# The prologue of a two-block network on one core, put into a fixed order: norm row spread by a product, first weight chunk ahead of token tile 1, decay logarithms after the prologue

## The chip, the core and the metric
The kernel runs on one core of a Trainium2 chip. Its five engines each work through a queue of their own in order: TensorE (PE, matrix products, with PEld for the loads of its stationary operand), VectorE (DVE), ScalarE (ACT), GpSimd (POOL) and SyncE (SP), which here does nothing but issue DMA transfers. The metric is the device time of one execution in microseconds (us); lower is better.

## The reference
256 tokens of width 1024 go through two different transformer blocks. All is float32. Only the first stage of the first block matters here: an RMS norm, a projection of the normed tokens with `w_in` (1024 x 3072), dilated window attention on one half of its columns, and retention on the other half.

```
def rms_norm(x, w, eps=NORM_EPS):
    xf = x.astype(jnp.float32)
    y = xf * lax.rsqrt(jnp.mean(xf * xf, axis=-1, keepdims=True) + eps)
    return (y * w.astype(jnp.float32)).astype(x.dtype)
...
def parallel_mixer(h, w_in, q_norm_w, k_norm_w, decay_f, decay_b, gn_w, w_out):
    proj = h @ w_in
...
    lg_f = jax.nn.log_sigmoid(decay_f.astype(f32))
    lg_b = jax.nn.log_sigmoid(decay_b.astype(f32))
    y_f = retention_chunkwise(qr, kr, vr, lg_f, inclusive=True)
...
x = x + parallel_mixer(rms_norm(x, norm_mix_w[l]), w_in[l], ...)
x = x + memory_cross_attention(...)
x = x + hierarchical_moe(...)
```

After it come a cross attention on a memory, a mixture of 32 experts (its weights are some 200 MB), and the second block: feed-forward, four-way mixer, feed-forward, twice.

## The kernel before, in words
The tokens are two tiles of 128 (`x[0]`, `x[1]`; tile 0 is called t0 here, tile 1 t1). A float32 product is made of three fast products: each operand is split into a high part and the remainder (`xh`, `xl` for the tokens, `wh`, `wl` for the weights), and `mm3` multiplies high by high, and each remainder by the other's high part (L310, L311, L312).

Weights come in chunks of 128 x 2048 elements (1 MB) through a ring of four buffers `raw`, in the order in which they are used. Each chunk has two halves of 1024 columns. For a half, ACT copies the high part (`wh`, L279) and DVE or POOL subtracts it (`wl`, L283). A counter `nw` in `weight` says who subtracts: POOL for each fourth half, DVE otherwise; the list `on_pool` overrules it (before, it sends both halves of the first chunk to POOL). The pools of `wh` and `wl` hold three halves each, so the high part of a half waits until TensorE has done with the half three before it.

`dense_nat` is one projection of both token tiles by 512 columns: two chunks, 2 tiles x 8 k-steps x 3 products = 48 matmuls of 128x128 by 512 columns. The first three are the keys, queries and values of the attention (chunks 0 and 1, 2 and 3, 4 and 5). When a key or query tile is done, `kdone` or `qdone` norms it by head (ACT square, DVE sum, POOL power -0.5 `rq`, DVE multiply) and TensorE transposes it (L401).

The prologue is `mixer1`: 18 products of zeros (`WARM`) keep TensorE busy while the loads run; SP issues x of t0 in two halves, the identity, x of t1, the norm row `norm_mix_w` copied from memory to all 128 partitions (0.5 MB into the core), and chunk 0 in two halves (512 KB each). Each tile is scaled by its 1/rms and the norm row (L530), transposed in two groups of four (L401) and split (L391, L392). `retention_start` then loads a row and the eight decays, and `log_decay` turns the decays into logarithms by a chain of some twenty small DVE operations, each waiting for the one before.

The framework's scheduler sets the order on each engine, except where `manual_schedule` takes the order of the code, and where `issue_after` ties one instruction behind another. Two groups of small constants are loaded meanwhile: for the router (`wr`, `tri`; POOL multiplies `wr`, DVE casts `tri`), and for a mixer of the second block (`bc_diff_lambda_2`, in `lambdas`: POOL product `lm`, DVE sum `ls`, ACT exponential). SP has eight completion semaphores (`DMAHW0` to `DMAHW7`) which it takes in turn, so an issue waits until the transfer eight before it has landed.

## Time and profile before

| | |
|---|---|
| median of 3 runs | 1740.98 us (1739.96 to 1743.69) |
| profiled execution, its own time | 1743.4 us |
| its span in the trace | 1741.7 us |
| TensorE busy | 1576.9 us (91%) |
| VectorE, ScalarE, GpSimd busy | 840.0, 656.5, 286.5 us |
| DMA moved | 419.07 MB |

The profile is of one execution; its own time is 1.7 us more than its span, and 2.4 us more than the median of the runs. A busy TensorE is not TensorE at its peak. Idle time of an engine costs only where another waits for it.

### The profile page before, as it was taken

The page shows a single profiled execution, that of the slowest core. Times are in us where ns is not written, and L with a number is a line of the kernel's source. Part 1 is how long each engine was busy: PE and PEld are TensorE (multiplying, and loading weights), DVE is VectorE, ACT ScalarE, POOL GpSimd, SP SyncE. Part 2 cuts the span into 40 slices and gives each one's busy share as a digit, 9 for nine tenths or more (in the row PEclk, how much of TensorE's full clock was granted, in tenths as well). Part 3 has the DMA queues.
Part 4 walks back from the last instruction along what each step waited for, and adds up shares of the span by engine and source line. Part 5 has one row for each costly group of instructions (what it writes and reads, how often), then busy time and mean ns, then how long its engine had stood idle before and what let it go on. Part 6 is the DMA issues. An engine that isn't in the chain of part 4 may idle for free.

```text
span 1741.7 us, 24950 instructions
## 1 busy us (share of the span) xinstructions
PE 1576.9 (91%) x10070; PEld 1215.4 (70%) x10070; DVE 840.0 (48%) x1468; ACT 656.5 (38%) x1125; POOL 286.5 (16%) x253
## 2 busy tenths in 40 slices
PE   8998998777776776999999989999999999989998
PEld 6777774322211221799988769999999988779997
DVE  5658653000000000554577775557654677765555
ACT  4655441000000000444545645444444536734442
POOL 4224312100000000312233250000100041330000
PEclk9999998987878886999999989999999999989999
DMA  7454959999999999855543235556455634145551
GB/s 278 149 185 142 359 192 422 417 421 421 420 421 421 421 420 421 318 194 192 195 171 135 79 145 194 184 180 241 148 191 193 243 105 147 50 179 190 179 190 72
DMA packets 66187, 419.07 MB, mean 241 GB/s; under 512 B 10641, under 2 KB 12177, under 8 KB 18705
## 3 DMA queue, kind: packets, MB, share of 16 engines
q1 hardware_dynamic: 66064, 417.39, 63.2%
q8 instruction: 82, 1.34, 0.3%
q14 instruction: 41, 0.33, 0.1%
HBM read 416.32 MB, written 1.05 MB: 240 GB/s over the span
## 4 chain that ended last, share of the span: by engine, by line
PE 63%; DMA 25%; DVE 4%; issue 4%; POOL 3%; ACT 1%; SPq 0%; DVEq 0%; POOLq 0%; ACTq 0%
DMA mraw<-in_wm 23%; PE ps L310 20%; PE ps L312 19%; PE ps L311 19%; PE ps L401 2%; PE ps L480 1%; POOL wl L283 1%; DMA raw<-in_wd 1%; DVE wl L283 1%; POOL rq L418 1%; DVE xa L1234 1%; ACT wh L279 0%; DMA bc_ln_g<-in_ln_g 0%; DVE xl L392 0%; PE ps L991 0%
## 5 line engine op out<-in xcount | busy, mean ns | idle before, releaser
L283 DVE TENSOR_TENSOR wl<-raw,wh 128x1024 fp32r<-128x1024 f32 (+2 forms) x314 | 388.9, 1249 | 292.3 <-ACT wh L279 289.4
L279 ACT ACTIVATE wh<-raw 128x1024 fp32r<-128x1024 f32 (+2 forms) x356 | 370.9, 1052 | 347.3 <-PE ps L311 177.5
L310 PE MATMUL ps<-xh,wh 128*128 128x256 f32 x1424 | 402.1, 282 | 3.4 <-ACT cv L1534 3.4
L312 PE MATMUL ps<-xh,wl 128*128 128x256 f32 x1424 | 401.3, 282 | 0.0
L311 PE MATMUL ps<-xl,wh 128*128 128x256 f32 x1424 | 401.1, 282 | 0.0
L310 PEld LDWEIGHTS ps<-xh,wh 128*128 128x128 f32 x1424 | 268.3, 188 | 7.0 <-ACT cv L1534 3.8
L311 PEld LDWEIGHTS ps<-xl,wh 128*128 128x128 f32 x1424 | 268.4, 188 | 1.8 <-issue 0.4
L312 PEld LDWEIGHTS ps<-xh,wl 128*128 128x128 f32 x1424 | 268.4, 188 | 0.8
L991 PE MATMUL ps<-mraw,xg 128*32 128x512 f32 x1024 | 168.2, 763 | 70.8 <-DMA mraw<-in_wm 70.6
L312 PE MATMUL ps<-wh,xl 128*128 128x512 f32 (+3 forms) x520 | 190.2, 370 | 6.5 <-DVE xl L392 6.3
L310 PE MATMUL ps<-wh,xh 128*128 128x512 f32 (+3 forms) x520 | 190.7, 376 | 4.7 <-ACT xh L391 3.8
L311 PE MATMUL ps<-wl,xh 128*128 128x512 f32 (+3 forms) x520 | 191.9, 370 | 2.2 <-POOL wl L283 1.1
L991 PEld LDWEIGHTS ps<-mraw,xg 128*32 128x32 f32 x1024 | 26.5, 119 | 200.4 <-DMA mraw<-in_wm 164.4
L418 POOL TENSOR_TENSOR rq<-rv,mhalf 128x1 f32<-128x1 f32 (+4 forms) x46 | 46.8, 1017 | 724.6 <-DVE rv L416 721.8
L283 POOL TENSOR_TENSOR wl<-raw,wh 128x1024 fp32r<-128x1024 f32 x42 | 103.2, 2463 | 279.5 <-ACT wh L279 180.4
L997 DVE TENSOR_TENSOR mf<-ps,mf 128x512 f32<-128x512 f32 x8 | 5.5, 692 | 238.7 <-PE ps L991 234.7
L312 PEld LDWEIGHTS ps<-wh,xl 128*128 128x128 f32 x520 | 100.8, 194 | 23.3 <-DVE xl L392 10.4
L310 PEld LDWEIGHTS ps<-wh,xh 128*128 128x128 f32 x520 | 101.0, 195 | 22.1 <-ACT xh L391 7.5
L311 PEld LDWEIGHTS ps<-wl,xh 128*128 128x128 f32 x520 | 101.4, 195 | 17.9 <-POOL wl L283 3.2
L312 PE MATMUL ps<-wh,hf 128*128 128x512 f32 x256 | 100.1, 391 | 0.0
L311 PE MATMUL ps<-wl,hf 128*128 128x512 f32 x256 | 100.1, 391 | 0.0
L310 PE MATMUL ps<-wh,hf 128*128 128x512 f32 x256 | 98.2, 390 | 0.0
(351 smaller groups left out, 1965.2 us busy)
## 6 DMA issues: line engine op xcount, KB each, us to landing
mraw<-in_wm SPq DMA_DIRECT2D x191, 1024.0 KB, 19.8
raw<-in_wd SPq DMA_DIRECT2D x179, 1024.0 KB, 4.9
raw<-in_wd SPq DMA_DIRECT2D x8, 512.0 KB, 11.0
raw<-in_wd SPq DMA_DIRECT2D x4, 832.0 KB, 4.4
bc_ln_g<-in_ln_g SPq DMA_DIRECT2D x6, 512.0 KB, 5.9
bc_ln_b<-in_ln_b SPq DMA_DIRECT2D x6, 512.0 KB, 6.6
raw<-in_wd SPq DMA_DIRECT2D x4, 768.0 KB, 4.4
bias<-in_bias SPq DMA_DIRECT2D x4, 512.0 KB, 6.5
```

Of the source, the lines that this page charges most:

```text
L279: s.nc.scalar.activation(h[:, :n], rc, AF.Copy)
L283: i = eng.tensor_tensor(l[:, :n], rc, h[:, :n].bitcast(F32), op=OP.subtract)
L310: mm(out, lhsT=lh, rhs=rh, start=start, stop=False)
L311: mm(out, lhsT=lh, rhs=rl, start=False, stop=False)
L312: mm(out, lhsT=ll, rhs=rh, start=False, stop=stop)
L401: s.nc.tensor.transpose(ps[:, b * 128:b * 128 + 128], src[:, b * 128:b * 128 + 128], s.ident)
L418: s.last_pow = s.nc.gpsimd.tensor_tensor(q, r, s.mhalf[:, :n], op=OP.pow)
L480: s.nc.tensor.matmul(out, lhsT=v(j), rhs=pt[:, 2 * i + j], start=first and j == 0, stop=last and j == 1)
L991: nc.tensor.matmul(ps[32 * e:32 * e + 32], lhsT=xg[:, k, 32 * e:32 * e + 32], rhs=w[:, e * FF:e * FF + FF], start=k == 0, stop=k == NK - 1 ...
L997: nc.vector.tensor_tensor(f, gu[1], f, op=OP.mult)
L1234: nc.vector.scalar_tensor_tensor(z[:, cs], z[:, cs], mv[:, 0:1], g[:, cs], op0=OP.subtract, op1=OP.mult)
```

## The change
1. The norm row is loaded as one row of 4 KB to one partition, and two products with a row of ones (K = 1, float32) put it on all partitions, in two PSUM banks `wn`. DVE reads it from there. The zeros' products are 14, the two products stand ahead of the last.
2. SP's order is new: x of t0, the row, the identity, the two loads of decays, chunk 0, then x of t1. The row `ret_gn_w` is loaded after the attention's code.
3. `norm1` writes the order of PE, ACT and DVE out by hand: t0's norm, transposes, chunk 0's splits (both `wl` halves now on DVE), 12 products of t0 with chunk 0, then tile 1's norm. The key projection goes on with chunk 1's first half for t0, and then t1.
4. `log_decay` is tied behind the last subtraction of the prologue (`norm1_end`), the product `qk` behind a power.
5. `nw` starts at -4 and the first chunk is not counted, so POOL gets the halves that are second to those it had: another half of each two chunks, up to the first feed-forward.

The core of the diff:

```
-        s.on_pool = [None, None]
+        s.on_pool = []
-        s.nw, s.pool_mod = 0, 4
+        s.nw, s.pool_mod = -4, 4
...
     def dense_nat(..., first=None):
+        if first:
+            w[0] = first(ps[0])
         if stagger:
             for t in range(NT):
-                for c in range(2):
+                for c in range(1 if first and not t else 0, 2):
                     part(t, c)
...
     def mixer1(s):
+                first, r = s.norm1(s.pool(c1, "rms1", side="right"), x, hs, lambda: s.retention_start(ctx))
+                o = s.xsplit()
+                with ExitStack() as c2:
+                    s.dilated(c2, hs, o, first)
+            r["lg"] = s.log_decay(r["p"], r["decay"])
+            r["gnw"] = s.bcast(r["p"], "ret_gn_w", 512)
...
+    def norm1(s, p, x, hs, small):
...
+        for cs in halves:
+            nc.sync.dma_start(x[0][:, cs], s.a["x"][:128, cs])
+        nc.sync.dma_start(row, s.a["norm_mix_w"])
+        nc.sync.dma_start(s.ident, s.a["ident"])
+        r = small()
+        raw = s.raw(cuts=2)
+        nc.sync.dma_start(x[1], s.a["x"][128:])
...
+        def tile(t, between):
+            q = s.rms_scale(z[t], x[t])
+            for c, cs in enumerate(halves):
+                nc.vector.scalar_tensor_tensor(z[t][:, cs], x[t][:, cs], q, wn[c], op0=OP.mult, op1=OP.mult)
+            tp = [s.transpose4(z[t][:, cs]).rearrange("p (b c) -> p b c", b=4) for cs in halves]
+            tk = slice(t * 128, t * 128 + 128)
+            between()
+            for c in range(2):
+                nc.scalar.activation(hs[0][:, 4 * c:4 * c + 4, tk], tp[c], AF.Copy)
+            for c in range(2):
+                h = hs[0][:, 4 * c:4 * c + 4, tk]
+                s.norm1_end = nc.vector.tensor_tensor(hs[1][:, 4 * c:4 * c + 4, tk], tp[c], h.bitcast(F32),
+                                                      op=OP.subtract)
+        def first(out):
+            with order:
+                for i in range(WARM):
+                    if i == WARM - 1:
+                        for c, cs in enumerate(halves):
+                            nc.tensor.matmul(wn[c], lhsT=one, rhs=row[:, cs], start=True, stop=True)
+                    nc.tensor.matmul(ps, lhsT=warm[:, :128], rhs=warm, start=True, stop=True)
+                tile(0, lambda: hi(0))
+                hi(1)
+                lo(0)
+                lo(1)
+                for a, b in ((0, 0), (1, 0), (0, 1)):
+                    for k in range(4):
+                        cs = slice(k % 2 * 512, k % 2 * 512 + 512)
+                        nc.tensor.matmul(out, lhsT=hs[a][:, k, :128], rhs=w[k // 2][b][:, cs], start=a + b + k == 0,
+                                         stop=False)
+                tile(1, lambda: None)
+            return w
...
+        s.issue_after(nc.gpsimd.tensor_tensor(qk, qw, kw, op=OP.mult), s.last_pow)
...
-        nc.vector.scalar_tensor_tensor(na, d, -1.0, d, op0=OP.mult, op1=OP.min)
+        s.issue_after(nc.vector.scalar_tensor_tensor(na, d, -1.0, d, op0=OP.mult, op1=OP.min), s.norm1_end)
```

First place: the head of SP's queue, from the program's start. Before (`raw_125` is chunk 0, `raw_264` chunk 1):

```order
L556 DMA x_91<-in_x 128x512 x2
L557 DMA ident_70<-in_ident 128x128
L558 DMA x_92<-in_x 128x1024
L238 DMA bc_norm_mix_w_123<-in_norm_mix_w 128x1024
L260 DMA raw_125<-in_wd 128x1024 x2
L260 DMA raw_264<-in_wd 128x2048
```

and of the change (`row_102` is the norm row, `raw_236` chunk 1):

```order
L580 DMA x_91<-in_x 128x512 x2
L581 DMA row_102<-in_norm_mix_w 1x1024
L582 DMA ident_70<-in_ident 128x128
L690 DMA decay_118<-in_ret_decay_f 128x4
L690 DMA decay_118<-in_ret_decay_b 128x4
L260 DMA raw_125<-in_wd 128x1024 x2
L585 DMA x_92<-in_x 128x1024 [waits DMAHW0_49]
L260 DMA raw_236<-in_wd 128x2048 [waits DMAHW1_49]
```

The norm row shrinks from 128 rows to one, the decays come ahead of chunk 0, and t1's tokens (`x_92`) behind it.

Second place: SP some transfers later, and DVE at the end of the prologue, where chunk 1's second half is subtracted. SP of the change, from chunk 3 (`raw_358`) on:

```order
L260 DMA raw_358<-in_wd 128x2048 [waits DMAHW7_49]
L666 DMA bias_496<-in_bias1 128x1024 [waits DMAHW0_49]
L666 DMA bias_497<-in_bias1 128x1024 [waits DMAHW1_49]
L238 DMA bc_ret_gn_w_772<-in_ret_gn_w 128x512 [waits DMAHW2_49]
L238 DMA bc_diff_lambda_2_774<-in_diff_lambda_2 128x128 [waits DMAHW3_49]
L867 DMA wr_1861<-in_w_route 128x8x37 [waits DMAHW4_49]
L871 DMA tri_1864<-in_tri 128x128 [waits DMAHW5_49]
```

DVE before, from the subtraction for chunk 1's first half (`wl_267`; its second half stands on POOL) to the first normed key tile (`qn_286`):

```order
L283 TENSOR_TENSOR wl_267<-raw_264,wh_266 128x1024 [waits DMAHW7_49,Activation_49]
L392 TENSOR_TENSOR xl_94<-ps_173,xh_93 128x4x128 [waits Activation_49]
L283 TENSOR_TENSOR wl_355<-raw_352,wh_354 128x1024 [waits DMAHW4_49,Activation_49]
L283 TENSOR_TENSOR wl_359<-raw_352,wh_358 128x1024 [waits Activation_49]
L426 TENSOR_REDUCE hss_288<-qn_286 128x8 [waits Activation_49]
L828 CAST trir_1863<-tri_1859 128x128 [waits DMAHW1_49]
L416 TENSOR_SCALAR rv_290<-hss_288 128x8 [waits DVE_49]
L283 TENSOR_TENSOR wl_389<-raw_386,wh_388 128x1024 [waits DMAHW5_49,Activation_49]
L586 TENSOR_TENSOR qn_286<-ps_242,rq_292 128x512 [waits Pool_49]
```

and of the change, from the prologue's last subtractions to the second half of chunk 1 (`wl_243`):

```order
L604 TENSOR_TENSOR xl_94<-ps_221,xh_93 128x4x128 [waits Activation_49]
L604 TENSOR_TENSOR xl_94<-ps_226,xh_93 128x4x128 [waits Activation_49]
L717 SCALAR_TENSOR_TENSOR lsna_742<-decay_118 128x8
L721 TENSOR_SCALAR lsw_746<-lsz_744 128x8 [waits Activation_49]
L722 RECIPROCAL lsw_746<-lsw_746 128x8 [waits DVE_49]
L723 TENSOR_TENSOR lsw_746<-lsw_746,lsz_744 128x8 [waits DVE_49]
L1259 TENSOR_REDUCE ls_778<-lm_776 128x2 [waits Pool_49]
L725 TENSOR_TENSOR lsw2_750<-lsw_746 128x8 [waits DVE_49]
L727 TENSOR_SCALAR lsacc_752<-lsw2_750 128x8 [waits DVE_49]
L875 CAST trir_1868<-tri_1864 128x128 [waits DMAHW5_49]
L729 TENSOR_TENSOR lsacc_752<-lsacc_752,lsw2_750 128x8 [waits DVE_49]
L283 TENSOR_TENSOR wl_243<-raw_236,wh_242 128x1024 [waits Activation_49]
```

The sum `ls` (behind POOL's `lm`, which waits for `bc_diff_lambda_2`) and the cast of `tri` now stand ahead of `wl_243`; before, the cast stood behind the subtractions for chunks 1 and 2, and the sum behind chunk 4's first half.

Third place: POOL in the retention, around the power `rq` of its first group norm. Before:

```order
L283 TENSOR_TENSOR wl_1658<-raw_1655,wh_1657 128x1024 [waits DMAHW4_49,Activation_49,Pool_49]
L283 TENSOR_TENSOR wl_1692<-raw_1689,wh_1691 128x1024 [waits DMAHW5_49,PE_49,Activation_49]
L283 TENSOR_TENSOR xw_1650<-raw_1733,xw_1650 128x1024 [waits DMAHW0_49,Activation_49]
L418 TENSOR_TENSOR rq_1553<-rv_1551,mhalf_71 128x4 [waits DVE_49]
L283 TENSOR_TENSOR wl_1696<-raw_1689,wh_1695 128x1024 [waits Activation_49]
L283 TENSOR_TENSOR wl_1726<-raw_1723,wh_1725 128x1024 [waits DMAHW6_49,Activation_49]
L418 TENSOR_TENSOR rq_1631<-rv_1629,mhalf_71 128x4 [waits DVE_49]
```

and of the change:

```order
L283 TENSOR_TENSOR wl_1663<-raw_1660,wh_1662 128x1024 [waits DMAHW4_49,Activation_49]
L283 TENSOR_TENSOR wl_1667<-raw_1660,wh_1666 128x1024 [waits Activation_49]
L283 TENSOR_TENSOR wl_1697<-raw_1694,wh_1696 128x1024 [waits DVE_49,DMAHW5_49,PE_49,Activation_49]
L283 TENSOR_TENSOR wl_1731<-raw_1728,wh_1730 128x1024 [waits DMAHW6_49,Activation_49]
L421 TENSOR_TENSOR rq_1558<-rv_1556,mhalf_71 128x4 [waits DVE_49]
L283 TENSOR_TENSOR wl_1735<-raw_1728,wh_1734 128x1024 [waits Activation_49]
L421 TENSOR_TENSOR rq_1636<-rv_1634,mhalf_71 128x4 [waits DVE_49]
```

Before, two subtractions stand right behind the first power (`rq_1553`), now one (`wl_1735` behind `rq_1558`); one more stands ahead of it.

## Rows read from the trace of the kernel before

**Rows 1.** The page, the chain that ended last: shares by engine.

```profile
PE 63%; DMA 25%; DVE 4%; issue 4%; POOL 3%; ACT 1%; SPq 0%; DVEq 0%; POOLq 0%; ACTq 0%
```

**Rows 2.** Windows: stretch, us, busy (x count) by engine, granted clock, DMA share, GB/s.

```profile
10.00:20.00 10.00, 8.16 (x28) 5.83 (x29) 6.84 (x9) 4.98 (x7) 7.50 (x7) 0.66 0.99 396
20.00:25.00 5.00, 5.00 (x23) 4.13 (x22) 1.35 (x2) 2.26 (x3) 3.76 (x5) 1.00 1.06 361
172.00:179.00 7.00, 5.66 (x23) 5.37 (x24) 6.03 (x8) 1.16 (x2) 3.51 (x2) 0.52 0.63 188
400.00:500.00 100.00, 73.66 (x414) 19.54 (x413) 6.50 (x18) 2.99 (x5) 3.85 (x5) 0.79 1.01 421
```

**Rows 3.** The chain in order of time, first 15 us: start, us, what.

```profile
3.19 8.63 DMA raw<-in_wd
11.84 1.07 ACT wh L279
12.98 2.43 POOL wl L283
```

**Rows 4.** Timeline of PE: start, us, instruction, count [idle before <- releaser].

```profile
1.60 5.97 PE L553 MATMUL ps<-warm 128*128 128x512 f32 x18 [1.60 <-DVE warm L550]
...
19.25 0.48 PE L312 MATMUL ps<-wh,xl 128*128 128x512 f32 x1
...
25.94 0.39 PE L311 MATMUL ps<-wl,xh 128*128 128x512 f32 x1
...
43.38 0.63 PE L401 MATMUL ps<-ident,qn 128*128 128x128 f32 x4 [0.68 <-DVE lsacc L684]
...
51.47 0.50 PE L311 MATMUL ps<-wl,xh 128*128 128x512 f32 x1 [0.91 <-POOL wl L283]
...
53.95 0.98 PE L507 MATMUL ps<-kt,qt 64*128 64x256 f32 x12
```

**Rows 5.** DMA issues of 0 to 19 us: count, KB each, us to landing.

```profile
ident<-in_ident SPq DMA_DIRECT2D x1, 64.0 KB, 3.2
x<-in_x SPq DMA_DIRECT2D x1, 512.0 KB, 6.2
raw<-in_wd SPq DMA_DIRECT2D x1, 1024.0 KB, 11.5
raw<-in_wd SPq DMA_DIRECT2D x1, 1024.0 KB, 8.4
tri<-in_tri SPq DMA_DIRECT2D x1, 64.0 KB, 8.4
```

**Rows 6.** Timeline of SP's DMA issues.

```profile
3.19 1.66 SPq L260 DMA_DIRECT2D raw<-in_wd  x3
...
10.32 1.85 SPq L260 DMA_DIRECT2D raw<-in_wd  x2
...
16.54 4.17 SPq L824 DMA_DIRECT2D tri<-in_tri  x1
```

**Rows 7.** Timeline of DVE and POOL, 10 to 27 us.

```profile
10.44 2.74 DVE L530 SCALAR_TENSOR_TENSOR rms<-x,rq,bc_norm_mix_w 128x512 f32<-128x512 f32 x4 [0.34 <-DMA bc_norm_mix_w<-in_norm_mix_w]
...
16.89 1.93 DVE L283 TENSOR_TENSOR wl<-raw,wh 128x1024 fp32r<-128x1024 f32 x1 [0.25 <-ACT wh L279]
...
24.34 1.23 DVE L283 TENSOR_TENSOR wl<-raw,wh 128x1024 fp32r<-128x1024 f32 x1 [3.48 <-ACT wh L279]
```

**Rows 8.** Groups of instructions, shapes apart: busy us, mean ns | idle before.

```profile
L1017 PE MATMUL ps<-my,gT 128*128 128x512 f32 x64 | 34.9, 674 | 9.0 <-ACT my L1015 9.0
```

**Rows 9.** Timeline of DVE, POOL and PE in the retention, 163 to 174 us.

```profile
163.15 2.49 DVE L731 TENSOR_SCALAR dtmp<-dist,lg 128x256 f32<-128x256 f32 x1
...
170.86 4.65 POOL L283 TENSOR_TENSOR wl<-raw,wh 128x1024 fp32r<-128x1024 f32 x2
...
170.92 4.67 DVE L715 TENSOR_SCALAR rn<-rn,rq 128x128 f32<-128x128 f32 x2 [0.87 <-POOL rq L418]
...
173.34 0.47 PE L401 MATMUL ps<-ident,rn 128*128 128x128 f32 x1 [1.63 <-DVE rn L715]
```

More of the change, by code (lines that the diff above doesn't have):

```diff
@@ L35 @@
 NAT, TAIL, PLACE = 2, 3, 4
-WARM = 18
+WARM = 14
 def _nat(w):
@@ L312, in mm3, with dense_nat @@
         mm(out, lhsT=ll, rhs=rh, start=False, stop=stop)
-    def dense_nat(s, x, n, done, stagger=False):
+    def dense_nat(s, x, n, done, stagger=False, first=None):
         xh, xl = x
@@ L544, in mixer1 @@
     def mixer1(s):
+        nc = s.nc
         x = [s.xp.tile([128, D], F32, name="x", tag=f"x{t}") for t in range(NT)]
@@ L547, in mixer1 @@
         with ExitStack() as ctx:
-            p = s.pool(ctx, "rms")
-            warm = p.tile([128, 512], F32R, name="warm")
-            s.nc.vector.memset(warm.bitcast(F32), 0.0)
-            ps = s.bank("mm")
-            for _ in range(WARM):
-                s.nc.tensor.matmul(ps, lhsT=warm[:, :128], rhs=warm, start=True, stop=True)
-            for c in range(2):
-                cs = slice(c * 512, c * 512 + 512)
-                s.nc.sync.dma_start(x[0][:, cs], s.a["x"][:128, cs])
-            s.nc.sync.dma_start(s.ident, s.a["ident"])
-            s.nc.sync.dma_start(x[1], s.a["x"][128:])
-            wn = s.bcast(p, "norm_mix_w", D)
-            s.ahead = [s.raw(cuts=2)]
-            for t in range(NT):
-                for c, z in s.rms(p, x[t], wn):
-                    s.tsplit(hs, t, z[:, c * 512:], k0=4 * c, n=4)
-        o = s.xsplit()
-        with ExitStack() as ctx:
-            r = s.retention_start(ctx)
-            with ExitStack() as c2:
-                s.dilated(c2, hs, o)
+            with ExitStack() as c1:
+                first, r = s.norm1(s.pool(c1, "rms1", side="right"), x, hs, lambda: s.retention_start(ctx))
[4 more added lines that the diff above has]
+            r["gnw"] = s.bcast(r["p"], "ret_gn_w", 512)
             s.lambdas(r["p"])
@@ L577, in mixer1 @@
         return x
+    def norm1(s, p, x, hs, small):
+        nc = s.nc
+        halves = [slice(c * 512, c * 512 + 512) for c in range(2)]
+        warm = p.tile([128, 512], F32R, name="warm")
+        nc.vector.memset(warm.bitcast(F32), 0.0)
+        one = p.tile([1, 128], F32, name="one")
+        nc.vector.memset(one, 1.0)
+        row = p.tile([1, D], F32, name="row")
+        for cs in halves:
[5 more added lines that the diff above has]
+        nc.sync.dma_start(x[1], s.a["x"][128:])
+        z = [p.tile([128, D], F32, name=f"z{t}") for t in range(NT)]
+        ps, wn = s.bank("mm"), [s.bank("b") for _ in range(2)]
+        w = [[s.wsp.tile([128, CH // 2], F32R, name=n, tag=n) for n in ("wh", "wl")] for _ in range(2)]
+        part = [raw[:, i * 1024:i * 1024 + 1024] for i in range(2)]
+        hi = lambda i: nc.scalar.activation(w[i][0], part[i], AF.Copy)
+        lo = lambda i: nc.vector.tensor_tensor(w[i][1], part[i], w[i][0].bitcast(F32), op=OP.subtract)
+        def tile(t, between):
[11 more added lines that the diff above has]
+                                                      op=OP.subtract)
+        order = s.tc.manual_schedule(engines={mybir.EngineType.PE, mybir.EngineType.Activation, mybir.EngineType.DVE})
+        def first(out):
[16 more added lines that the diff above has]
+            return w
+        return first, r
@@ L589, in head_normed, with dilated @@
         return y
-    def dilated(s, ctx, hs, o):
+    def dilated(s, ctx, hs, o, first):
         nc, a = s.nc, s.a
@@ L637, in retention_start @@
         r["gate"] = [p.tile([128, 512], F32, name=f"rg{t}") for t in range(NT)]
-        r["gnw"] = s.bcast(p, "ret_gn_w", 512)
-        r["lg"] = s.log_decay(p)
+        d = r["decay"] = p.tile([128, 8], F32, name="decay")
+        for i, n in enumerate(("ret_decay_f", "ret_decay_b")):
+            v = s.a[n]
+            s.nc.sync.dma_start(d[:, 4 * i:4 * i + 4], bass.AP(tensor=v.tensor, offset=v.offset, ap=[[0, 128], [1, 4]]))
         for i in range(2):
@@ L660, in retention_proj, with log_decay @@
         s.dense_nat(hs, 512, rgdone)
[L662 removed]
+    def log_decay(s, p, d):
         nc = s.nc
[L665 to L668 removed]
         na = p.tile([128, 8], F32, name="lsna")
[L670 removed]
+        s.issue_after(nc.vector.scalar_tensor_tensor(na, d, -1.0, d, op0=OP.mult, op1=OP.min), s.norm1_end)
         z = p.tile([128, 8], F32, name="lsz")
```

8 lines of the change are left out of this document (1 added, 7 removed).

## The prediction
> **What bounds the kernel now.** I first read the page's chain, the work that ended last: 63% of the span is TensorE and 25% transfers [rows 1]. The windows say where the transfers rule: from 400 to 500 us the queues are busy all the time at 421 GB/s [rows 2]. That stage streams the experts' weights, and each buffer is reloaded when TensorE has used it, so it starts as early as the work before it ends. A prologue shorter by 1 us makes the execution 1 us shorter, unless a later stall eats it.
>
> In the first 20 us the chain is chunk 0: its load takes 8.63 us from 3.19, ACT's high part 1.07, POOL's subtraction 2.43 [rows 3]. TensorE has its zeros from 1.60 to 7.57 and is at 0.66 of its clock on the mean of 10 to 20 us, which mixes its two levels (1.2 and 2.4 GHz); from 20 it has the whole clock [rows 2, 4]. From 19.25 to 25.94 it streams 29 products at 0.23 us, and then 38 of the 48 key products are done (counted along its queue). The remaining 106 of the three projections, with three groups of transposes, end at 53.95: 28.0 us, where 106 x 0.23 are 24.4. Two stalls explain 1.59 of the difference: 0.68 at 43.38 (the decay chain, `lsacc`, holds DVE's queue) and 0.91 at 51.47 (POOL's `wl`) [rows 4].
>
> **The change, part by part.** I follow the new order with those durations; landings are issue plus time to land.
>
> *Norm row.* Instead of 0.5 MB, 4 KB come in. Two more float32 products of 512 columns are, by another float32 product's group, 0.67 us each [rows 8]: 1.35, against four zeros taken out (4 x 5.97/18 = 1.33). Bounds: nothing, and 1.35 on the path. I take nothing: the cover is chunk 0's load. The row stands on all partitions about 8 us from the start, the scaling of tile 0 takes 2 x 0.69 [rows 7], and the high part of chunk 0 is not there before 9.3 (next). DVE's product of the decays stands ahead of this scaling, so their landing counts too: issued about 3.2, after 3.2 (as the identity) or 6.2 us (as x of t1) [rows 5], at 6.4 to 9.4. The late end would add 1.9; I take the early one, since the load is small like the identity.
>
> *Chunk 0.* It goes ahead of t1's tokens. Issued about 3.7, half a chunk should land between 6.9 and 9.9, by the same two rows; I take 8.2, for it stands behind 0.5 MB of t0's tokens. Before it was 11.82 [rows 3]. High parts at 9.3 and 10.4, and DVE's subtractions (1.23 each [rows 7], where POOL took 2.43) at 11.7 and 12.9. The 12 products of t0 with it end behind the last subtraction, 12.9 + 4 x 0.35 (0.23 at a clock of 0.66) = 14.3.
>
> *Chunk 1.* It was the third issue of the group at 3.19 to 4.85, say at 4.3, and landed 11.5 later, 15.8 [rows 5, 6]. Half a megabyte less at 396 GB/s [rows 2] makes 14.5. High part 15.6, subtraction 16.8 (DVE), scaling of t1 18.2; transposes and splits bring TensorE to t1 about 19.4. Of the key products 36 should be done about 23.1 to 24.5, the latter if the clock is still at its lower level. Before, at 23.1, it was 26. So the gross lead is 10 products, 2.3 us.
>
> *Given back on DVE.* Its queue now holds the sum for the lambdas and the cast of `tri` ahead of `wl_243`, the second half of chunk 1. SP issues their loads behind both biases, and the second bias waits for chunk 1's landing (its semaphore). So `tri` is issued at 14.5 to 15.8 and lands 8.4 later [rows 5], up to 24.2, with 3 MB ahead of it in the queue; I take that end. Then `wl_243` (1.23) ends about 25.6 and TensorE gets its 39th key product at 25.8, where before it had it at 25.94 [rows 4]. Two query products are then already done (0.46). The lead is 0.6: the transfer, not TensorE, sets this place.
>
> *Behind it.* TensorE next needs `wl_327`, directly behind on DVE, while POOL subtracts `wl_331`. A subtraction of DVE beside POOL's took 1.93 for 1.23 [rows 7], and in the retention two small operations took 4.67 beside POOL's 4.65 [rows 9]. By the two the loss is 0.7 to 2.4; I take 1.5, since POOL starts first. The Trainium skill (SBUF — State Buffer, "SBUF: two separate sides") calls the pair of ports that the two share an exclusive lock, held for the whole instruction; the retention's rows agree (DVE waited POOL's pair out), and by it the loss would be up to 2.4 and the sum 0.9 worse. For the rest, the decay chain is now done before it can block a norm, and DVE has both halves of chunk 5, so the stalls of 43 and 51 us should go: 25.8 + 104 x 0.23 + 1.05 (three groups of transposes, an estimate of 0.35 each) + 1.5 = 52.3, against 53.95. Lead at the end of the projections: 1.6.
>
> *Retention.* POOL has one subtraction instead of two behind the first `rq`, 2.3 less. DVE's second operation beside it comes free earlier, but TensorE waited 1.63 for the first alone [rows 9]. Nothing to 2.3; I take 0.6, as the first one stays blocked. The qk product, the later `ret_gn_w` and the 0.5 MB less cost nothing: TensorE and POOL's norms cover them, with 10 us and more between them. Without that cover a 256 KB row would cost its 7 us or so, an estimate between ident's and `tri`'s rows.
>
> Sum: 1.6 + 0.6 = 2.2 on the profiled execution's own 1743.4: 1741.2. That execution is 2.4 above the median of 1740.98, so the forecast of the median is **1738.8**.
>
> **The rivals.** *The lead is kept (faster).* If the small loads land within some 6 us, as x of t1 did (6.2 [rows 5]), `tri` is there at 22, DVE gets to `wl_243` before TensorE asks, and the gross 2.3 stay. With the stalls of 43 and 51 us gone (1.6) and 0.6 from the retention it is 4.5: a median of 1736.5. If TensorE's wait in the retention also stays short enough for the clock to hold (it was at 0.52 from 172 to 179, after the idle time; 0.48 x 7 = 3.4 us [rows 2, 9]), 1733.1. Against it: loads of 1 MB took 8.4 to 11.5 there, and the small `tri` as long.
>
> *The lead is eaten (no change).* The decays are two loads of 16 bytes for each of 128 partitions, ahead of chunk 0 in the queue. If their many packets hold it for some 2 us, or if the wait before 25.8 lowers TensorE's clock (12 products at 0.23 more are 2.8), the lead of 2.2 is gone: 1741.0. For it: TensorE had been idle 3.7 us before the stretch at 0.66. Against the packets: four columns of one value per partition lie between chunks 1 and 2, which landed at 15.8 and 18.7 [rows 5, 6], 2.9 apart, where 1.05 MB at 396 GB/s alone take 2.65; all four cost 0.25. The Trainium skill (DMA: Bandwidth & Descriptors, "Bandwidth") gives 0.67 us for 4 KB in 64 packets, about 10.5 ns a packet; for the decays' 256 rows that would be an estimate of 2.7 us, and the lead of 2.2 would become a loss of 0.5. The trace disagrees: a column load of 64 packets or more cost some 0.06 here.
>
> *Slower.* In the retention one more subtraction, `wl_1731`, stands on POOL ahead of `rq_1558`. If it starts just before its operand is ready, the power is up to 2.4 us late, TensorE waits 1.63 + 2.4, and its clock is lowered earlier and for longer. That is 2.4 + 1.5 (4 us more of a stretch at 0.52 to 0.66) + the 0.6 not gained: 4.5 against the 2.2, or a median of 1743.3; with the lock costing its 2.4 at `wl_327`, 1744.2, and where the decays' chain or a key norm is held as well, 1745. It decides from a power that comes 2 us later than before on. For it: DVE's and POOL's pieces are long there, 2.49 for one `dtmp` [rows 9]. Against it: the load `raw_1728` must be there by then.
>
> **How the numbers follow.** Forecast case 0.42 (1737 to 1740.5), lead kept 0.30 (1733 to 1737.4), eaten 0.13 (1740 to 1742), slower 0.15 (1743 to 1746). A measurement of this kernel can tell about 0.2%, 3.5 us, from no change: faster is under 1737.5, slower over 1744.5. Faster: all of the second case and a quarter of the first, 0.40; slower: most of the last, 0.13; no change 0.47. The range, 1734.0 to 1743.5, leaves out the clock that holds in the retention and the later half of the slower case. The likeliest case's own range is 1737 to 1740.5.
>
> **What would show it.** Right: chunk 0 lands about 8.2 and TensorE's first weight product stands at 9.5 to 10; chunk 1 lands about 14.5; the cast of `tri` and with it `wl_243` wait until 23 to 24.2, TensorE until 25.8; no wait on `lsacc` at 43; projections done about 52; one `rn` of about 2.3 and a short one. Wrong: `wl_243` done before 24 (the lead is larger), a first weight product after 11 (decays or norm row on the path), a granted clock below 1 behind 26 us, a power `rq_1558` that starts over 2 us later beside its operand.

## The result, and the profile after

The change makes the kernel slower: 1753.04 us (1747.85 to 1755.23, 5 runs) against 1741.09 us (1739.96 to 1743.69, 5 runs), a ratio of 1.0058 with an interval of 1.0047 to 1.0069, or 12 us. The forecast was 1738.8 us, and its range ended at 1743.5. The profiled execution took 1755.23 us by its own time, the slowest of the five, its span 1753.6 us.

The prologue itself did what was forecast. Four views of the changed kernel answer to [rows 4, 5, 7]. First TensorE's timeline, with the rows on which the steps end:

```profile
7.04 1.98 PE L613 MATMUL ps<-row,one 1*128 1x512 f32 x4
...
10.65 1.22 PE L622 MATMUL ps<-wh,xh 128*128 128x512 f32 x2
...
25.86 0.50 PE L311 MATMUL ps<-wl,xh 128*128 128x512 f32 x1 [0.38 <-DVE wl L283]
...
29.34 0.50 PE L311 MATMUL ps<-wl,xh 128*128 128x512 f32 x1 [0.89 <-DVE wl L283]
...
52.12 0.36 PE L310 MATMUL ps<-xh,wh 128*128 128x256 f32 x1
```

Then ACT and DVE, the two operations that wait for chunk 0 and for `tri`, and the subtraction behind the cast:

```profile
9.06 1.06 ACT L590 ACTIVATE wh<-raw 128x1024 fp32r<-128x1024 f32 x1 [3.93 <-DMA raw<-in_wd]
...
23.97 0.62 DVE L875 CAST trir<-tri 128x128 fp32r<-128x128 f32 x1 [0.20 <-DMA tri<-in_tri]
...
24.59 1.21 DVE L283 TENSOR_TENSOR wl<-raw,wh 128x1024 fp32r<-128x1024 f32 x1
```

and the issues of the first 19 us with their time to land:

```profile
ident<-in_ident SPq DMA_DIRECT2D x1, 64.0 KB, 2.6
tri<-in_tri SPq DMA_DIRECT2D x1, 64.0 KB, 7.9
...
decay<-in_ret_decay_f SPq DMA_DIRECT2D x1, 2.0 KB, 4.9
```

The norm row's products end at 9.02, chunk 0 is there for ACT at 9.06 (11.84 before), the cast of `tri` starts at 23.97, and chunk 1's second half comes off DVE at 25.80, so that TensorE goes on at 25.86 (forecast 25.8). The three projections and the third group of transposes are over at 52.1, where they took until 53.95. The lead of 1.8 us is there, and it is lost behind it.

Where it goes, the windows show (columns as in [rows 2]). The kernel before:

```profile
54.00:100.00 46.00, 43.54 (x296) 35.16 (x296) 28.00 (x80) 29.33 (x69) 7.49 (x5) 1.00 0.52 186
...
150.00:200.00 50.00, 43.37 (x203) 34.94 (x202) 40.49 (x72) 22.60 (x38) 17.49 (x10) 0.93 0.59 217
...
700.00:760.00 60.00, 56.83 (x446) 49.79 (x445) 32.87 (x39) 27.90 (x41) 15.96 (x6) 1.00 0.75 277
```

and the changed kernel:

```profile
54.00:100.00 46.00, 40.12 (x255) 30.97 (x254) 25.93 (x78) 26.33 (x64) 6.92 (x4) 0.96 0.47 162
...
150.00:200.00 50.00, 41.45 (x188) 33.36 (x187) 37.32 (x71) 21.28 (x35) 15.17 (x9) 0.90 0.51 176
...
700.00:760.00 60.00, 52.85 (x387) 41.12 (x386) 27.64 (x32) 23.25 (x34) 16.67 (x6) 0.95 0.78 296
```

TensorE is busy 3.4 us less in the attention (54 to 100), 1.9 less in the retention, both at a lower mean clock, and 4.0 less where the first feed-forward begins; in the last stretch most of that is delay that arrives there (the experts' last product ends at 717.6, before at 708.0). Its new waits in the attention, and behind the memory's keys, in its timeline:

```profile
87.66 0.65 PE L499 MATMUL ps<-pt,va 128*64 128x256 f32 x2 [1.75 <-ACT pt L476]
...
153.63 0.74 PE L404 MATMUL ps<-ident,mqn 128*128 128x128 f32 x4 [1.11 <-DVE mqn L817]
165.08 0.50 PE L310 MATMUL ps<-wh,xh 128*128 128x512 f32 x1 [2.29 <-ACT mv L808]
```

and two loads that are late on SP, first the changed kernel and then, for the second of them, the one before:

```profile
68.34 0.33 SPq L260 DMA_DIRECT2D raw<-in_wd  x1
68.90 0.33 SPq L666 DMA_DIRECT2D bias<-in_bias  x1
...
154.44 0.33 SPq L743 DMA_DIRECT2D dist<-in_dist  x1
```

```profile
147.41 0.33 SPq L696 DMA_DIRECT2D dist<-in_dist  x1
```

The retention's distances `dist` are loaded 7.0 us later, into a buffer of the memory's key projection, behind its last transposes. The bias for the attention's second group of heads was issued from 65.35 on before; its second half now has a weight chunk ahead of it and took 8.69 us in the chain.

Not only the waits moved. Counted along TensorE's queue, the transposes of the norms stand behind these numbers of weight products:

```
                        query, key norms        memory's keys
before                  82 109 134 187          418 444 470 492
changed                 84 114 144 192          417 450 480 498
before, new halves (e2) 85 114 144 192          417 450 480 498
```

The third row is the kernel before with one number changed: which half of the weights POOL subtracts. That is point 5 of the change.

### The profile page after: what moved, and what is told of

Same layout as the page of the kernel before. It is cut to its first block, busy times and chain, and to the rows that moved or that the text cites. A ratio compares the mean times of both kernels' runs of the same rounds, so it can differ in the third digit from the quotient of the medians.

```text
span 1753.6 us, 24955 instructions
## 1 busy us (share of the span) xinstructions
PE 1583.5 (90%) x10070; PEld 1219.1 (70%) x10070; DVE 839.7 (48%) x1471; ACT 657.1 (37%) x1125; POOL 279.1 (16%) x251
## 4 chain that ended last, share of the span: by engine, by line
PE 65%; DMA 24%; DVE 5%; ACT 2%; issue 2%; POOL 1%; SPq 0%; DVEq 0%; ACTq 0%; POOLq 0%
DMA mraw<-in_wm 23%; PE ps L310 20%; PE ps L312 19%; PE ps L311 19%; PE ps L404 2%; PE ps L483 1%; PE ps L1038 1%; DVE xa L1281 1%; DVE wl L283 1%; POOL rq L421 1%; DMA raw<-in_wd 1%; DMA bias<-in_bias 0%; ACT wh L279 0%; DVE dtmp L778 0%; DMA tri<-in_tri 0%
## 5 line engine op out<-in xcount | busy, mean ns | idle before, releaser
L283 DVE TENSOR_TENSOR wl<-raw,wh 128x1024 fp32r<-128x1024 f32 (+2 forms) x313 | 382.8, 1233 | 291.5 <-ACT wh L279 290.3
```

Of the source, the lines that this page charges most:

```text
L283: i = eng.tensor_tensor(l[:, :n], rc, h[:, :n].bitcast(F32), op=OP.subtract)
```

## The experiments

Eighteen kernels. The theory that I held after the first trace was that the halves given to POOL, not the prologue, turned the order behind it; the rivals were the new prologue itself, the two late loads, and the small operations on DVE. Medians, and ratios to the kernel before as it was measured beside each (its medians were 1741.09 beside the changed kernel and 1741.64 to 1742.76 beside the others):

| run | median, us | ratio, 95% interval |
|---|---|---|
| changed kernel | 1753.04 | 1.0058 (1.0047 to 1.0069) |
| e1 halves back | 1751.18 | 1.0051 (1.0034 to 1.0068) |
| e2 before, new halves | 1754.30 | 1.0062 (1.0046 to 1.0079) |
| e3 bias early | 1751.51 | 1.0051 (1.0034 to 1.0067) |
| e4 distances early | 1747.25 | 1.0027 (1.0017 to 1.0038) |
| e5 small loads late | 1750.43 | 1.0050 (1.0033 to 1.0066) |
| e6 halves back, chunk 1 on DVE | 1744.90 | 1.0015 (1.0006 to 1.0025) |
| e7 before, distances early | 1743.09 | 1.0008 (0.9998 to 1.0017) |
| e8 three edits | 1748.07 | 1.0039 (1.0025 to 1.0053) |
| e9 new prologue, clean | 1745.27 | 1.0016 (1.0007 to 1.0025) |
| e10 old prologue, clean | 1748.04 | 1.0034 (1.0022 to 1.0046) |
| e11 halves back from chunk 5 | 1745.24 | 1.0016 (1.0006 to 1.0025) |
| e12 no POOL to chunk 5 | 1744.48 | 1.0010 (1.0001 to 1.0020) |
| e13 the same, distances early | 1743.28 | 1.0009 (1.0000 to 1.0018) |
| e14 the same, bias early | 1743.88 | 1.0009 (1.0000 to 1.0018) |
| e15 norms first | 1741.44 | 0.9998 (0.9989 to 1.0007) |
| e16 the same, distances early | 1741.53 | 1.0000 (0.9991 to 1.0009) |
| e17 key places back | 1746.45 | 1.0029 (1.0019 to 1.0038) |
| e18 all places back | 1745.45 | 1.0022 (1.0013 to 1.0031) |

**Which part of the change: the halves (e1, e2, e6, e11).** The edits: e1 and e2 set the counter's start in the changed kernel and in the kernel before, e6 also keeps chunk 1 off POOL, e11 goes back to the old halves from chunk 5 on.

```
e1, e6  -        s.nw, s.pool_mod = -4, 4
        +        s.nw, s.pool_mod = -2, 4
e2      -        s.nw, s.pool_mod = 0, 4
        +        s.nw, s.pool_mod = -2, 4
e6      -  (s.pool_mod and s.nw % s.pool_mod == 0)
        +  (s.pool_mod and s.nw > 0 and s.nw % s.pool_mod == 0)
e11     -  (s.pool_mod and s.nw % s.pool_mod == 0)
        +  (s.pool_mod and (s.nw + 2 * (s.nw > 4)) % s.pool_mod == 0)
```

> The changed kernel with one number put back: the counter nw starts so that POOL again subtracts the second half of chunks 1, 3 and 5, as in the kernel before. Halves theory (which half POOL gets changes the order behind the prologue, and that order costs some 14 us): the loss goes, and the prologue's lead of about 2 us shows, 1737 to 1741 us; TensorE's wait of 1.75 for the softmax and the late bias load (68.9) and distance load (154.4) are back near 67 and 147. Waits-of-the-prologue theory (the new prologue itself upsets the attention): it stays at 1750 to 1755.

> The kernel before with one number changed: POOL gets the halves that the change gives it (second of chunks 2 and 4), all else as before. Halves theory: slower by most of what the change lost, 1750 to 1757 us, with the distance load issued some 5 us later. Prologue theory: within 3 us of 1741.

> The changed kernel with POOL's halves as before (second of chunks 3, 5, ...) but chunk 1 wholly on DVE, so that no subtraction of the prologue waits on POOL behind the router's and the lambdas' loads as in the run with the halves put back. Halves theory: with that wait gone the order behind the prologue is near that of before and the lead shows: 1738 to 1743 us. If the new prologue loses in the attention whatever the halves: 1747 or more.

> The changed kernel, in which POOL keeps the change's halves in chunks 2 and 4 and goes back to those of before from chunk 5 on; the transposes of queries and of the memory's keys then stand behind as many products as before (134, 187, 418 to 492). If the places of the transposes are what costs: 1743 to 1747 us, most of the loss gone. If POOL's own work in chunks 2 and 4 costs: 1750 or more.

e2 came out as the halves theory had it: with the old prologue and the new halves the kernel loses 11.7 us, all that the change lost. e1 missed: putting the halves back in the changed kernel gained little (its interval and the changed kernel's overlap). POOL's half is then chunk 1's second, and stands on POOL behind the lambdas' product, which waits for its load. DVE's small `lsacc` is held 2.33 us beside it, and TensorE waits 3.63 us for the subtraction that stands behind that on DVE. POOL and TensorE in e1:

```profile
22.80 0.32 POOL L1257 TENSOR_TENSOR lm<-bc_diff_lambda 128x64 f32<-128x64 f32 x1 [7.52 <-DMA bc_diff_lambda<-in_diff_lambda]
...
24.31 2.36 POOL L283 TENSOR_TENSOR wl<-raw,wh 128x1024 fp32r<-128x1024 f32 x1
...
28.98 0.65 PE L311 MATMUL ps<-wl,xh 128*128 128x512 f32 x1 [3.63 <-DVE wl L283]
```

With chunk 1 on DVE (e6) that goes, and the loss falls from 12 to 3.2 us. e11, with the change's halves in chunks 2 and 4 and the old ones from chunk 5 on, comes to the same place, 2.5: most of the cost is in the halves behind chunk 4. Both have the transposes of queries and keys at 134, 187 and 418 to 492 again. The windows of e6 are close to those of the kernel before, and those of e2 to those of the changed one (e6 first):

```profile
54.00:100.00 46.00, 43.44 (x288) 34.71 (x287) 27.82 (x79) 30.12 (x71) 6.95 (x4) 0.99 0.50 170
150.00:200.00 50.00, 43.38 (x201) 34.95 (x200) 40.91 (x73) 23.93 (x40) 17.53 (x10) 0.93 0.58 208
```

```profile
54.00:100.00 46.00, 40.19 (x267) 31.03 (x266) 26.40 (x78) 28.05 (x65) 6.95 (x5) 1.00 0.48 170
150.00:200.00 50.00, 41.47 (x188) 33.39 (x187) 37.33 (x71) 21.07 (x35) 15.46 (x10) 0.90 0.51 179
```

TensorE's busy time between 54 and 100 is 43.5 and 43.4 with the old halves, 40.1 and 40.2 with the new ones, whichever prologue stands ahead.

**By what: the places of the transposes, or POOL's own work (e17, e18).** Both moved together so far. These two keep the change's halves and tie the products behind the transposes, so that the scheduler must put the keys' transposes where they were, and in e18 the queries' too, the second of them further ahead than it was (168 products for 187).

```
+            s.np += 1
+            if s.np in s.gates:
+                s.issue_after(i, s.turned[s.gates[s.np]])
e17     +        s.gates = {products 445 to 469: the second key transposes, 471 to 491: the third, 493 to 519: the fourth}
e18     as e17, and products 135 to 168: the first query transposes, 188 to 229: the second
```

> The changed kernel, POOL's halves untouched, with the products behind the transposes of the memory's keys tied so that these transposes stand behind 444, 470 and 492 products as before, not behind 450, 480 and 498. Place theory (the scheduler's later places make the distances' load and the retention late): 2.5 to 6 us less, 1747 to 1750.5, with the distances loaded 2 to 3 us earlier. Halves theory (POOL's work at another time holds DVE and the norms themselves): TensorE waits at the earlier places instead, within 1.5 us of 1753.

> The same with the query norms' transposes moved forward too, to 134 and 168 products (144 and 192 in the changed kernel, 134 and 187 before). Place theory: another 2 to 4 us less, 1744 to 1748. Halves theory: within 1.5 us of 1753, with new waits of TensorE at the transposes.

e17 puts the keys' transposes at 444, 470 and 492, and its median gives 7.2 of the 12 us back, with POOL's halves as the change has them. That is the time that the place theory named; its mechanism is not what the trace shows. The first and the fourth of these transposes, in the kernel before, in the changed kernel (the fourth is shown above, at 153.63) and in e17:

```profile
128.46 0.60 PE L401 MATMUL ps<-ident,mqn 128*128 128x128 f32 x4
...
146.74 0.60 PE L401 MATMUL ps<-ident,mqn 128*128 128x128 f32 x4
```

```profile
132.49 0.60 PE L404 MATMUL ps<-ident,mqn 128*128 128x128 f32 x4
```

```profile
130.15 0.60 PE L409 MATMUL ps<-ident,mqn 128*128 128x128 f32 x4
...
151.21 0.74 PE L409 MATMUL ps<-ident,mqn 128*128 128x128 f32 x4 [0.82 <-DVE mqn L823]
```

From the first to the fourth it is 18.3 us before, 21.1 in the changed kernel, and 21.1 in e17 with the places back. The third norm was ready at its earlier place; the fourth was not, and TensorE waits for it. Its power stands on POOL behind a subtraction of the new halves, though its operand was ready at 146.48. POOL in e17:

```profile
146.53 2.38 POOL L284 TENSOR_TENSOR wl<-raw,wh 128x1024 fp32r<-128x1024 f32 x1 [5.72 <-issue]
148.86 1.68 POOL L427 TENSOR_TENSOR rq<-rv,mhalf 128x2 f32<-128x2 f32 x1
```

The distances' load of e17 is 2.5 us earlier than the changed kernel's (151.98), but 2.3 of that is there at the first of these transposes, ahead of all that the edit ties. Up to there the two kernels have the same order on every engine, and in both TensorE waits 1.75 us for the same softmax at 87 us. Behind that wait it ran at about half its clock in the changed kernel's profiled execution, and at the whole clock in e17's (and in e4's, which has the same TensorE order). The window of the changed kernel, then e17's:

```profile
88.00:92.00 4.00, 4.00 (x21) 3.77 (x20) 0.13 (x1) 0.00 (x0) 0.00 (x0) 0.57 0.53 218
```

```profile
88.00:92.00 4.00, 4.00 (x36) 3.52 (x36) 0.00 (x0) 1.72 (x3) 0.00 (x0) 1.00 0.30 123
```

The rest of e17's gain stands in the retention, whose order the tie changed too: TensorE's clock, at half its speed for a part of the retention in the changed kernel, stays up there (0.97 at 150 to 200, where the changed kernel has 0.90):

```profile
150.00:200.00 50.00, 44.82 (x213) 35.23 (x212) 38.55 (x75) 24.34 (x40) 18.25 (x11) 0.97 0.64 240
```

e18 is 1.0 us below e17, with intervals that overlap, where 2 to 4 were expected. Its query transposes stand earlier in the queue but hardly in time (51.47 and 60.25 us; 51.77 and 60.60 in the changed kernel), since TensorE now waits 0.69 and 1.92 us at them: the sign that was named for the halves theory. So it is shown that the new halves cost most of the 12 us; that they do it by the places of the transposes alone is not.

Where the lateness arises can be read from the profiled executions. Lateness against the kernel before, in us: at the first and the fourth key transposes, at the next transposes of that kind (the memory's queries, at 219.42 before), at the end of the experts' products (708.0 before), and at the end:

```
                      first key  fourth key  queries  experts' end  end
changed                  4.0        6.9        8.7        9.6       11.9
before, new halves (e2)  3.6        6.5        8.2        9.0       11.3
halves back (e6)         2.2        2.3        2.2        2.1        2.1
distances early (e4)     2.0        4.8       -0.7       -0.3        0.9
key places back (e17)    1.7        4.5        0.8        1.1        2.9
```

Each row is one execution. In the changed kernel and in e2 the lateness grows in four places: the attention, the memory's keys, the retention and the first feed-forward. With the old halves (e6) it does not grow behind the attention; e4 and e17 make up in the retention what they lost ahead of it.

**The late loads (e3, e4, e7).** e3 has four bias buffers and ties the second group's loads behind chunk 5; e4 and e7 give the distances a tile of their own, loaded behind the retention's last chunk in program order.

```
e3      -  bias = [p.tile([128, 2, 2, S], F32, name="bias", tag="bias", bufs=2) for _ in HALVES]
        +  bias = [p.tile([128, 2, 2, S], F32, name="bias", tag="bias", bufs=4) for _ in HALVES]
        +  if g: s.issue_after(i, s.last_dma)
e4, e7  +  r["dist"] = r["p"].tile([128, 2, 2, S], F32, name="dist")
        +  s.issue_after(s.nc.sync.dma_start(r["dist"], s.a["dist"]), s.last_dma)
```

> The changed kernel with four bias buffers, so that the second group's two bias loads go out behind chunk 5 and not at 67 and 69 us. If the late bias (DVE waited 4.3 us for it, and TensorE 1.75 and 1.41 us behind, with 3.4 us at half clock) costs what the chain says: 3 to 5 us less, 1748 to 1750. If the softmax is late for another reason (ACT's and DVE's queues): within 1.5 us of 1753.

> The changed kernel with the retention's distances in a tile of their own that is loaded long before, so that the decay factors need not wait for a buffer of the memory's key projection. If the late load (154.4 for 147.4 us) sets the retention's end: 2 to 5 us less, 1748 to 1751. If the retention is late because its inputs and engines are late anyway: within 1.5 us of 1753.

> The kernel before with the distances in a tile of their own, loaded long before the retention. If their late load costs in every order, as it did in the changed kernel (6 us): 2 to 5 us less than before, 1737 to 1740. If the 7 us by which the change delayed the load were the whole cost: within 1.5 us of 1742.

For the bias nothing is shown: 3.1 us less by the differences to the kernel before, with intervals that overlap, and TensorE still waits 1.25 for a softmax there. The distances were part of it: 7.4 us less in the changed kernel, none in the kernel before (+1.3, its interval reaches to no change). So a late load costs only in the order that makes it late. The 7.4 are not the load's 7.0 us of delay handed on: e4 is still 4.8 us late at the fourth key transposes and makes it up in the retention, where TensorE is not slowed (a granted clock of 1.00 over 150 to 200).

**What the prologue is worth, and what took it (e5, e8 to e16).** e5 and e8 tie the small loads behind chunk 5; e9 and e10 tie instead the operations that read them behind the last query norm, and let POOL have no half of chunks 1 to 4, with the new prologue and the old one. e8 has the small loads late, e6's halves and the early distances. e12 to e14 leave chunk 5 off POOL too. e15 and e16 are e9 with the subtractions from chunk 6 on tied behind the first query norm.

```
e5, e8   +  s.issue_after(<load of wr, tri, diff_lambda_2>, s.late)      # the raw of chunk 5
e9, e10  +  s.issue_after(<cast of tri, sum ls>, s.late[0])              # the last query norm
         +  s.issue_after(<products wr, lm on POOL>, s.late[1])          # its power
e9       +  (s.pool_mod and s.nw > 4 and s.nw % s.pool_mod == 0)         # with nw from -2
e10      +  (s.pool_mod and s.nw > 8 and s.nw % s.pool_mod == 0)         # with nw from 0
e12-e14  +  (s.pool_mod and s.nw > 8 and s.nw % s.pool_mod == 0)         # with nw from -2
e15, e16 +  if s.hold: s.issue_after(<subtraction>, s.hold)              # the first query norm
```

> The changed kernel with the loads for the lambdas, the router and the triangle tied behind chunk 5, so that DVE's cast and sum no longer stand ahead of chunk 1's second half; TensorE's order is the same. If the lead that DVE gave back there (TensorE held to 25.8 and 29.3 us) carries to the end: 1.5 to 3 us less, 1750 to 1751.5. If the attention's chain behind it, and not TensorE, sets the pace: within 1 us of 1753.

> The changed kernel with three edits at once: small loads tied behind chunk 5, POOL's halves as before with chunk 1 on DVE, distances loaded early. If the three costs are separate: the lead of 2 to 4 us and the distances' 2 to 4 show, 1734 to 1738, faster than both kernels. If they are one cost seen in three ways, or the order turns against it: 1741 or more.

> The changed kernel with three things put behind the prologue or back: POOL's halves as before but none in chunks 1 to 4, and DVE's and POOL's operations for the lambdas, the router and the triangle tied behind the last query norm. Two-causes theory (the halves' order cost some 8 us, the small operations 2 to 3, DVE's wait on POOL's port at 47 us the rest): the new prologue's lead shows, 1736 to 1740 us. If a third part of the change costs something behind the prologue: 1742 or more.

> The kernel before with the same two edits (no half on POOL in chunks 1 to 4, small operations tied behind the last query norm): what is left between it and the changed kernel so edited is the prologue alone. If the prologue is worth 2 to 4 us there: 1739 to 1743 us, and the other run 2 to 4 below it. If the edits make the gain: both the same within 1 us.

e5 leaves TensorE's order as it is and takes away only what DVE waited for at 24 us: 3.3 us less by the differences to the kernel before, 2.6 by the medians. The intervals overlap, so the times do not show that this lead carries to the end; in the trace it is there at the first query transposes (49.26 for 51.77) and at the first key transposes (128.52 for 132.49, where some 2 us are the clock at 88 to 92). e9 and e10 have the same halves and differ in points 1 to 4 of the change: 2.8 us for the new prologue, as expected. But both are slower than the kernel before, and e8 too missed; it has several waits of 0.9 to 1.9 us, which no run takes apart. In e9 and e10 the edits had opened a new wait. POOL, DVE and TensorE in e9:

```profile
46.80 2.35 POOL L283 TENSOR_TENSOR wl<-raw,wh 128x1024 fp32r<-128x1024 f32 x1
```

```profile
46.82 3.41 DVE L283 TENSOR_TENSOR wl<-raw,wh 128x1024 fp32r<-128x1024 f32 x1 [1.74 <-ACT wh L279]
50.16 0.68 DVE L635 TENSOR_TENSOR qn<-ps,rq 128x512 f32<-128x512 f32 x1
```

```profile
50.98 1.04 PE L404 MATMUL ps<-ident,qn 128*128 128x128 f32 x4 [3.48 <-DVE qn L635]
```

POOL starts 0.02 us ahead of DVE, and DVE's 1.2 us become 3.41; the norm behind it on DVE is late, and TensorE waits 3.48 for its transposes. e6, e10 and e11 have the same wait (3.49, 3.44 and 3.48). This was tried in two ways:

> As the run of the new prologue with both edits, but POOL gets no half of chunk 5 either. There TensorE waited 3.48 us for the first query norm, since DVE's subtraction took 3.41 instead of 1.23 beside POOL's half of chunk 5. Port theory: that wait goes and the time falls by 2 to 4 us, to 1741 to 1743. If the norm's place in TensorE's order is what costs (it now stands behind 144 products instead of 134): no gain, 1745 or more.

> The run before this one with the distances loaded early as well. If the retention still waits for them: 2 to 4 us less than that run, 1738 to 1741, below the kernel before. If their load is late only with the change's halves, as the kernel before showed: within 1.5 us of that run.

> The same run with four bias buffers instead. If the second group's scores wait for their bias (68 us and later): 1 to 3 us less, 1739 to 1741.5. If the scores are late by themselves: within 1 us.

> The run of the new prologue with both edits (POOL's halves as before but none in chunks 1 to 4, small operations behind), in which DVE's subtractions from chunk 6 on are tied behind the first query norm, so that the norm no longer stands behind a subtraction that waits for POOL's port. If the 3.48 us wait at 47 us is what took the prologue's lead: it goes, and the time is 2.5 to 5 us below that run, 1740 to 1743, at or below the kernel before. If DVE and ACT in the attention set the end anyway: within 1.5 us of 1745.

> The same with the distances loaded early. Late-load theory: another 1 to 2 us, 1738 to 1741, faster than both kernels. Otherwise: as the run before it within 1 us.

e12 takes the wait away and gains 0.5 us: the transposes moved from 134 to 144 and the next from 187 to 198, and waits of 1.1 to 1.3 us came back at 58, 60 and 87 us. It told nothing apart. Early distances or bias add 1.2 and 0.6, no more than the intervals leave open. e15 keeps POOL's half and moves the norm ahead of the subtraction; the second query's transposes move too, from behind 187 products to behind 170. It takes 2.7 us less than e9, level with the kernel before. POOL, DVE and TensorE in e15:

```profile
46.90 2.36 POOL L284 TENSOR_TENSOR wl<-raw,wh 128x1024 fp32r<-128x1024 f32 x1
46.96 0.69 DVE L639 TENSOR_TENSOR qn<-ps,rq 128x512 f32<-128x512 f32 x1 [1.78 <-POOL rq L424]
...
47.57 2.77 DVE L284 TENSOR_TENSOR wl<-raw,wh 128x1024 fp32r<-128x1024 f32 x1
47.80 0.63 PE L407 MATMUL ps<-ident,qn 128*128 128x128 f32 x4 [0.20 <-DVE qn L639]
```

The norm, which reads PSUM and POOL's small result, is not held up beside the same POOL instruction; the subtraction behind it is (2.77). e16 adds nothing. No version was faster than the kernel before.

## Why the prediction was wrong

Its terms for the prologue held: norm row and decays at no cost (the scaling of tile 0 starts at 8.26, within the cover), chunk 0 at 9.06 where 8.2 was taken (bounds 6.9 to 9.9), chunk 1 there for ACT at 14.24 (14.5), the cast of `tri` at 23.97 (up to 24.2), TensorE at 25.86 (25.8), the projections done at 52.1 (52.3), the stalls of 43 and 51 us gone. And e9 against e10 gives the prologue 2.8 us, where the sum had a lead of 1.6. Mis-sized were terms that the next wait covered: the norm row's two products took 1.98 us (1.35), the first weight product came at 10.65 (9.5 to 10), and the 12 products of t0 ended at 17.1 (14.3), since DVE's splits of t0 stand ahead of chunk 0's subtractions; t1 still came at 19.6 (19.4). `wl_327`, priced at 1.5, cost 0.89 at 29.34, and not as the sum had it: what POOL's subtraction held was an operation of the decay chain ahead of it on DVE.

```profile
25.79 2.37 DVE L730 TENSOR_SCALAR lsacc<-lsacc 128x8 f32<-128x8 f32 x1
```

The step that failed is the pricing of point 5 of the change, POOL's other halves. The prediction priced them at one place, the retention's first `rq`, with 0.6 us of gain, and at nothing everywhere else. "A prologue shorter by 1 us makes the execution 1 us shorter, unless a later stall eats it" left room for a later stall, but I looked for it among the stalls of the trace of before. The halves reach the scheduler and the engines everywhere up to the first feed-forward. Measured, the term that the sum lacked is 11.7 us with the halves alone in the kernel before (e2), and 8.8 come back with the old halves, and chunk 1 on DVE, in the changed kernel (e6).

How the halves cost this is shown in part. The scheduler answered them by putting most of the transposes of the norms 2 to 10 products later in TensorE's queue, and each of these norms goes through one buffer, so the next can't start before the transposes of the last one. But at the old places TensorE waits (e17, e18), once for a norm whose power is held behind POOL's subtraction. Of the 7.0 us by which the distances' load is late, 4.0 are there at the first key transposes and 2.9 arise from there to the fourth, with the places back or not. In the first feed-forward it is the halves themselves: POOL's subtraction starts 0.7 us ahead of DVE's, which takes 2.73 us, and TensorE waits 2.29 for it, where before it waited 0.78 at this place; e2, e4 and e17 have the same wait (2.31, 2.30, 2.30), e6 has 0.78. POOL, DVE and TensorE in the changed kernel:

```profile
720.22 2.36 POOL L283 TENSOR_TENSOR wl<-raw,wh 128x1024 fp32r<-128x1024 f32 x1 [79.55 <-DVE x L987]
720.94 2.73 DVE L283 TENSOR_TENSOR wl<-raw,wh 128x1024 fp32r<-128x1024 f32 x1
...
723.72 0.58 PE L311 MATMUL ps<-wl,xh 128*128 128x256 f32 x1 [2.29 <-DVE wl L283]
```

The retention's term fell with the rest. Two `rn` beside one subtraction took 2.56 for the 4.67 of [rows 9], as forecast, but the whole stage was over 8 us late. The slower rival had the place and one mechanism right, `wl_1731` ahead of the power. POOL and DVE in the changed kernel:

```profile
176.08 2.40 POOL L283 TENSOR_TENSOR wl<-raw,wh 128x1024 fp32r<-128x1024 f32 x1 [7.14 <-ACT wh L279]
178.58 1.01 POOL L421 TENSOR_TENSOR rq<-rv,mhalf 128x4 f32<-128x4 f32 x1
```

```profile
176.67 1.83 DVE L419 TENSOR_SCALAR rv<-gmv 128x4 f32<-128x4 f32 x1
```

The power starts at 178.58, 8.7 later than [rows 9] lead one to expect, but by far the most of that was there before POOL's subtraction began; what the rival named is DVE's small `rv`, 1.83 us, held until POOL was done. Its price was not what happened: TensorE's two waits there are 2.14 and 1.64 us, where they were 1.90 and 1.63.

In e15 the first query norm's transposes come at 47.8 (49.9 before), the second's at 56.1 (60.1 before), and yet the attention ends when it did. The trace shows where the lead goes: at 61 us TensorE is still 1.9 ahead, and then it waits 2.00 us for a subtraction on DVE and runs at 0.57 of its clock. DVE had waited for the lambdas' second product on POOL, which waited 4.50 us for its load; these are the small operations that e9 to e16 tie behind the last query norm. TensorE in e15, and its window:

```profile
64.52 0.50 PE L314 MATMUL ps<-wl,xh 128*128 128x512 f32 x1 [2.00 <-DVE wl L284]
```

```profile
64.50:68.50 4.00, 3.98 (x10) 3.12 (x11) 2.87 (x14) 2.19 (x8) 0.00 (x0) 0.57 0.90 350
```

No run takes that wait away, so what the prologue would gain without it is not known. Left open is also by what step the new halves cost their 3.6 us in the attention (e2): neither the places (e18) nor the bias (e3) is shown to be it.

## What to carry to other kernels

Where a scheduler writes the order, the edit that looks like bookkeeping (which engine takes which piece) can cost more than the edit that the change is about: here 9 to 12 us against a gain of 2.8. Before pricing, look in the new order at what stands ahead of each step of a serial chain (norm, power, transposes, next norm), on the waiting engine and above all on the engine that got other pieces: here a subtraction of 2.4 us ahead of a small power. No stall in the old trace shows it. And an A/B of a mixed change should undo the bookkeeping first: one number put into the old kernel (e2) showed at once which part of the change took the time. A place moved back, though, moves more than the place: read in the trace whether the step came earlier before the time is put down to it.

## What the runs showed of the hardware

Beside a POOL subtraction that began 0.02 us ahead of it, a DVE subtraction of 1.2 us took 3.41 (e9), and TensorE waited 3.48 us behind it. Beside other such subtractions DVE operations on 128x8 and 128x4 elements took 2.37 and 1.83; a DVE multiply from PSUM took its usual 0.69 (e15). The Trainium skill (SBUF — State Buffer, "SBUF: two separate sides") gives the pair of ports that POOL shares with a DVE operation in a two-port mode, or with two operands in SBUF, to whichever starts first, for the whole instruction. These rows agree with it.

The granted clock decides how much an idle stretch costs. The changed kernel waited for the distances and the norms of the retention, and from 180 to 190 us it ran at 0.53, most of it at the lower of the two levels (1.2 GHz):

```profile
180.00:190.00 10.00, 7.60 (x27) 6.39 (x28) 6.46 (x18) 2.04 (x5) 2.91 (x2) 0.53 0.68 239
```

In e4 (distances loaded at 57.85) and e17 the same stage, with shorter waits ahead of it, kept 1.00 and 0.97 over 150 to 200 us. And the same wait does not always cost the clock: behind the 1.75 us at 87 us, with the same order on TensorE, the clock was 0.57 over 88 to 92 in the changed kernel's execution and 1.00 in e4's and e17's. That alone is 2.1 to 2.3 us between executions, so a gain read from one profile is set against the medians.

Two loads of 2 KB (the decays) took 4.7 to 4.9 us to land, the 64 KB of the identity, issued just ahead, 2.6; I had taken the identity's time for them.
